# Newton steps and q/k scaling of a layer moved from VectorE to GpSimd

## The chip, the cores and the metric

The kernel runs on one core of a Trainium2 chip. The metric is the device time of one execution in microseconds (us). The core's engines work side by side, each through its own queue in order: TensorE (PE in the profile, its weight loads PEld), VectorE (DVE), ScalarE (ACT), GpSimd (POOL) and SyncE (SP, which only issues transfers). They are tied together by semaphores. GpSimd also issues transfers of its own.

## The reference, cut to what matters

Two pre-norm transformer layers over 512 tokens of width 1024, everything in fp32: layer 0 with stick-breaking attention, layer 1 with differential attention, each followed by a SwiGLU feed-forward of width 2816. The change lies in layer 1, in its two inner RMS norms.

```python
q = rms_norm(q.reshape(b, s, 8, 2, 64), q_g)     # 8 heads, two halves of 64 each
k = rms_norm(k.reshape(b, s, 8, 2, 64), k_g)
q1, q2, k1, k2 = ...                             # the halves, first 16 of 64 rotated by position
a = softmax(q1 k1 / 8) - lam * softmax(q2 k2 / 8)  # block-causal in chunks of 64
o = a @ v                                        # 128 wide per head
o = rms_norm(o, sub_g) * (1 - lam_init)
x = x + o @ w_out
```

## The kernel before

Every matrix product is done in three passes on a high and a low part of each operand (`mm3`), so that fp32 accuracy is kept. Activations lie transposed (features on partitions) between the layers; weights come in tiles of 128x1024.

Layer 1 (`diff_layer`) works in four chunks of two heads. For each chunk `qk_steps` multiplies out q and k with the tokens on partitions (`ps_nat`, four token tiles of 512 columns), ScalarE copies each into `qk_nat` (128x2048 in all) and squares it, and VectorE sums the squares of each group of 64 into `qk_ss` (128x32). Then, once for each chunk, the inverse roots of these 32 sums are found by `rsqrt`: a first guess from the bit pattern and three Newton steps of three VectorE instructions each, and the whole 128x2048 is multiplied by them (L773). GpSimd rotates the first 16 of each 64 (`rope`, L790 to L793). `v_steps` makes v for the same two heads. `head_stacks` transposes q and k of one head on TensorE (L802), splits them into high and low parts, and has GpSimd copy the k parts to the other partitions by a transfer (L334).

A head (`head`, `attend`, `weights`) does its scores in four query tiles: scores on TensorE, maximum on VectorE (L815), exponential on ScalarE (L816), the difference of the two softmaxes on VectorE (L828, two inputs in SBUF), transposes on TensorE (L358) and a split into high and low (L361, L362), then the product with v. `head_out` norms one head's output: transposes (L860), squares and sums on ScalarE (`o_sq`, L865), on VectorE a threshold factor `fin` (L873, L874) and the inverse root of four sums per partition (`rsqrt` on 128x4), their product (L877), the scaling of the transposed output from PSUM (L878), transposes back (`tb`, L887) and the split into `ohi` and `olo` (L890, L891). It is called inside the next head, behind that head's first query tile; for the eighth head after everything.

The matrix products of chunks 1 to 3 (and in heads 6 and 7 the first half of the output projection, `out_first`) are handed out in small steps between the query tiles, so that TensorE has work while a head waits. What is written is not the final order: a planner puts the instructions of each engine in an order by a simulated time line, in which earlier written work goes first when it is ready. On the chip that order is kept on each engine, whatever comes late. `tmp`, `sm` and PSUM tiles are reused in turn.

The change touches the end of `qk_steps` (L770 to L775) and the middle of `head_out` (L873 to L877), and adds a second inverse root beside `rsqrt` (L139).

Of the kernel before, what the change touches and what calls it, by code (L numbers as in the profile page):

```python
# [12 lines left out]
F32 = mybir.dt.float32  # L13
F32R = mybir.dt.float32r
BF16 = mybir.dt.bfloat16
I32 = mybir.dt.int32
AF = mybir.ActivationFunctionType
ALU = mybir.AluOpType
# [3 lines left out]
P = 128  # L22
# [4 lines left out]
TT = S // P  # L27
# [5 lines left out]
RSQRT_MAGIC = float(0x5F3759DF)  # L33
# [10 lines left out]
def trunk(  # L44
# [27 lines left out]
    V, A, G, T = nc.vector, nc.scalar, nc.gpsimd, nc.tensor  # L72

    const = ctx.enter_context(tc.tile_pool(name="const", bufs=1))
# [4 lines left out]
    sm = ctx.enter_context(tc.tile_pool(name="sm", bufs=4))  # L79
# [53 lines left out]
    def wload_kept(key):  # L133
        hi, lo = pair()
        nc.sync.dma_start(out=hi.bitcast(F32), in_=kept[key][0])
        nc.sync.dma_start(out=lo.bitcast(F32), in_=kept[key][1])
        return hi, lo

    def rsqrt(v, n):  # L139
        u = sm.tile([P, 32], F32, tag="rs_u", name="rs_u")[:, :n]  # L140
        t = sm.tile([P, 32], F32, tag="rs_t", name="rs_t")[:, :n]
        V.tensor_scalar(
            u.bitcast(I32), v.bitcast(I32), -0.5, RSQRT_MAGIC, op0=ALU.mult, op1=ALU.add
        )
        for _ in range(3):
            V.scalar_tensor_tensor(t, u, -0.5, u, op0=ALU.mult, op1=ALU.mult)
            V.tensor_tensor(t, t, v, op=ALU.mult)
            V.scalar_tensor_tensor(u, t, 1.5, u, op0=ALU.add, op1=ALU.mult)
        return u

    class Norm:
# [97 lines left out]
    def nat_steps(ws, h, evac, cols, n):  # L249
        per = 1024 // cols  # L250
        for t in range(TT):
            ts_ = slice(t * P, (t + 1) * P)
            ps = mm.tile([P, S], F32, tag="mm", name="ps_nat")[:, :cols]
            for k in range(KT):
                w = ws[k // per]
                c = slice((k % per) * cols, (k % per + 1) * cols)
                mm3(
                    ps,
                    (h[k][0][:, ts_], h[k][1][:, ts_]),
                    (w[0][:, c], w[1][:, c]),  # L260
                    k == 0,
                    k == KT - 1,
                )
                if (k + 1) % (KT // n) == 0 and k < KT - 1:
                    yield
            evac(t, ps)
            yield
# [443 lines left out]
    def diff_layer(norm, nxt):  # L711
        h = norm.h
        with ExitStack() as st:
# [14 lines left out]
            def norm_ready():  # L728
                if not norm.done:
                    norm.finish(tnp, "tn")  # L730
                    V.tensor_scalar_mul(rsv, norm.rstd, phi)
# [22 lines left out]
            def qk_steps(c, out):  # L754
                t_ = qp.tile([P, TT, S], F32, tag="qk", name="qk_nat")
                ss = sm.tile([P, 32], F32, tag="rs_v", name="qk_ss")

                def evac(t, ps):
                    norm_ready()
                    A.activation(t_[:, t], ps, AF.Copy, scale=norm.rstd[:, t : t + 1])  # L760
                    sq = tmp.tile([P, S], F32, tag="tmp", name="qk_sq")
                    A.activation(sq, t_[:, t], AF.Square)
                    V.reduce_sum(
                        ss[:, t * 8 : (t + 1) * 8],
                        sq.rearrange("p (g d) -> p g d", d=64),
                        axis=AX.X,
                    )

                yield from nat_steps([wload_kept(("wqk", c, j)) for j in range(4)], h, evac, 512, 2)
                V.tensor_scalar(ss, ss, 1.0 / 64, EPS, op0=ALU.mult, op1=ALU.add)  # L770
                u = rsqrt(ss, 32)
                f3 = t_.rearrange("p t (g d) -> p (t g) d", d=64)
                V.tensor_tensor(  # L773
                    f3, f3, u.unsqueeze(2).to_broadcast([P, 32, 64]), op=ALU.mult
                )  # L775
                for which in range(2):
                    f4 = t_[:, :, which * 256 : which * 256 + 256].rearrange(
                        "p t (g d) -> p t g d", d=64
                    )
                    ta, tb = (  # L780
                        r.unsqueeze(2).to_broadcast([P, TT, 4, ROT]) for r in rot[which]
                    )
                    mt = tmp.tile([P, S], F32, tag="tmp", name="rope")
                    m = [
                        mt[:, i * 256 : i * 256 + 256].rearrange(
                            "p (t g d) -> p t g d", t=TT, d=ROT
                        )
                        for i in range(2)
                    ]
                    G.tensor_tensor(m[1][:, :, :, 0:8], f4[:, :, :, 8:16], tb[:, :, :, 0:8], op=ALU.mult)  # L790
                    G.tensor_tensor(m[1][:, :, :, 8:16], f4[:, :, :, 0:8], tb[:, :, :, 8:16], op=ALU.mult)
                    G.tensor_tensor(m[0], f4[:, :, :, 0:ROT], ta, op=ALU.mult)
                    G.tensor_tensor(f4[:, :, :, 0:ROT], m[0], m[1], op=ALU.add)  # L793
                out.append(t_)
# [53 lines left out]
                    )  # L848
                return av, ss

            def head_out(av, ss):
                ho = raw_tile()
                ot, on = ho[:, :S], ho[:, S:]
                A.activation(ot, av, AF.Copy)
                rs = sm.tile([P, TT], F32, tag="rs1", name="rs1")
                V.reciprocal(rs, ss[:, 0])
                tp = tnp.tile([P, S], F32, tag="tn", name="tn")
                for t in range(TT):
                    o = (TT - 1 - t) * P
                    T.transpose(tp[:, t * P : (t + 1) * P], ot[:, o : o + P], ident)  # L860
                v = sm.tile([P, 32], F32, tag="rs_v", name="o_ss")[:, :TT]
                sq = tmp.tile([P, S], F32, tag="tmp", name="o_sq")
                for t in range(TT):
                    c = slice(t * P, (t + 1) * P)
                    A.activation(  # L865
                        sq[:, c],
                        tp[:, c],
                        AF.Square,
                        scale=rs[:, t : t + 1],
                        accum_out=v[:, t : t + 1],  # L870
                    )
                fin = sm.tile([P, TT], F32, tag="fin", name="fin")
                V.tensor_scalar(fin, v, thr, None, op0=ALU.is_lt)  # L873
                V.tensor_tensor(fin, fin, rs, op=ALU.mult)  # L874
                V.tensor_scalar(v, v, 1.0 / P, eps_phi, op0=ALU.mult, op1=ALU.add)
                u = rsqrt(v, TT)
                V.tensor_tensor(u, u, fin, op=ALU.mult)  # L877
                V.tensor_tensor(  # L878
                    on.rearrange("p (t d) -> p t d", d=P),
                    tp.rearrange("p (t d) -> p t d", d=P),  # L880
                    u.unsqueeze(2).to_broadcast([P, TT, P]),
                    op=ALU.mult,
                )
                tb = tnp.tile([P, S], F32, tag="tn", name="tb")
                for t in range(TT):
                    c = slice(t * P, (t + 1) * P)
                    T.transpose(tb[:, c], on[:, c], ident)  # L887
                hi = hp.tile([P, S], F32R, tag="t", name="ohi")
                lo = hp.tile([P, S], F32R, tag="t", name="olo")
                A.activation(hi, tb, AF.Copy, scale=gs)  # L890
                V.scalar_tensor_tensor(  # L891
                    lo, tb, gs, hi.bitcast(F32), op0=ALU.mult, op1=ALU.subtract
                )
                og.append((hi, lo))
# [9 lines left out]
            after = nothing  # L904
# [7 lines left out]
            for hd in range(8):  # L912
                hh = hd % 2
                c = hd // 2

                def middle():
                    if hd < 7:
                        if hh == 1:
                            flush(gens["qk", c + 1])
                        stacks.append(head_stacks(qk[(hd + 1) // 2], (hd + 1) % 2))  # L920

                def before():
                    if c > 0:
                        flush(gens["v", c])
                    if hd == 6:
                        fillers.append(last)

                q2, k2 = stacks[hd]
                av, ss = head(hh, q2, k2, lambda: vs[c], after, middle, counts[hd], before)
                after = partial(head_out, av, ss)  # L930
            after()
            flush()
            banks = [(mm, "mm"), (mm, "mm"), (scp, "sc"), (scp, "sc"), (tqp, "tq"), (tpp, "tp"), (mm, "mm"), (mm, "mm")]
# [90 lines left out]
```

## Time and profile before

| | |
|---|---|
| runs | median 1266.99 us of 3 (1265.03 to 1267.15) |
| profiled execution | 1268.86 us, span 1267.0 us |
| PE busy in the span | 1225.4 us, 97% |
| DVE / ACT / POOL busy | 732.2 / 566.8 / 101.4 us |
| chain that ended last | PE 89%, DVE 3%, issue 3%, DMA 3%, ACT 1% |

The profile shows one execution. The span runs from the first to the last instruction; 1.86 us of the execution lie around it. Times of rows are us from the start of the span, durations of single instructions in us or ns as the view says. Layer 1's attention stage, with the norms that the change touches, lies between about 640 and 890 us.

### The profile page before, as it was taken

To read this page: it belongs to the slowest core of one execution; us is meant where nothing else is said; L and a number is where in the kernel's file an instruction comes from. 1 tells how busy PE (TensorE), PEld (TensorE's weight loads), DVE (VectorE), ACT (ScalarE), POOL (GpSimd) and SP (SyncE) were. 2 spreads that over 40 slices of the span, in tenths; PEclk is the share of its full clock that TensorE was granted. 3 is DMA by queue.
4 is the path that set the end of the run, shared out by engine and by line. 5 is a ranking of instruction groups with operands and counts; after the bars stand their busy time and mean duration, and the time that the engine had idled before them with its cause. 6 is when DMAs were issued, how large, how long until landed. Compare 5 with 4: busy or idle time off the path is not lost.

```text
span 1267.0 us, 16005 instructions
## 1 busy us (share of the span) xinstructions
PE 1225.4 (97%) x5974; PEld 1024.5 (81%) x5974; DVE 732.2 (58%) x1396; ACT 566.8 (45%) x962; POOL 101.4 (8%) x169
## 2 busy tenths in 40 slices
PE   7899999989999999999999999987999999999998
PEld 6788888768888888888888998775888888888886
DVE  6467777677654555455633777885754434443442
ACT  7687977555432333233423555554442222222320
POOL 2211112001111111001101201100000000000000
PEclk9899999999999999999999999999999999999999
DMA  6966848236867776767645463531333233322222
GB/s 205 218 124 152 182 102 199 67 106 222 270 227 248 242 226 234 252 236 234 241 184 184 150 212 99 179 100 34 106 111 98 87 100 100 100 89 95 96 75 79
DMA packets 60397, 198.39 MB, mean 157 GB/s; under 512 B 8288, under 2 KB 9312, under 8 KB 60320
## 3 DMA queue, kind: packets, MB, share of 16 engines
q1 hardware_dynamic: 41760, 138.90, 34.3%
q0 software_dynamic: 18416, 58.47, 17.0%
q8 instruction: 47, 0.77, 0.2%
q14 instruction: 30, 0.25, 0.1%
q10 hardware_dynamic: 144, 0.01, 0.0%
HBM read 153.31 MB, written 35.65 MB: 149 GB/s over the span
## 4 chain that ended last, share of the span: by engine, by line
PE 89%; DVE 3%; issue 3%; DMA 3%; ACT 1%; POOL 0%; SPq 0%; DVEq 0%; POOLq 0%; ACTq 0%
PE ps_d L216 6%; PE ps_d L217 6%; PE ps_d L218 6%; PE ps_u L216 6%; PE ps_g L216 6%; PE ps_u L218 6%; PE ps_g L217 6%; PE ps_u L217 6%; PE ps_g L218 6%; PE ps_nat L216 4%; PE ps_nat L217 4%; PE ps_nat L218 4%; PE ps_o L216 2%; PE ps_o L217 2%; PE ps_o L218 2%
## 5 line engine op out<-in xcount | busy, mean ns | idle before, releaser
L109 ACT ACTIVATE whi<-wraw 128x1024 fp32r<-128x1024 f32 (+1 forms) x138 | 140.6, 1034 | 344.2 <-PE ps_d L217 82.4
L110 DVE TENSOR_TENSOR wlo<-wraw,whi 128x1024 fp32r<-128x1024 f32 (+1 forms) x138 | 164.2, 1191 | 93.7 <-ACT whi L109 47.5
L216 PE MATMUL ps_u<-hhi,whi 128*128 128x512 f32 x352 | 137.9, 392 | 3.5 <-DVE k L679 3.5
L217 PE MATMUL ps_d<-alo,whi 128*128 128x512 f32 x352 | 138.9, 396 | 0.0
L218 PE MATMUL ps_d<-ahi,wlo 128*128 128x512 f32 x352 | 138.9, 396 | 0.0
L216 PE MATMUL ps_d<-ahi,whi 128*128 128x512 f32 x352 | 138.7, 396 | 0.0
L216 PE MATMUL ps_g<-hhi,whi 128*128 128x512 f32 x352 | 137.5, 392 | 0.0
L218 PE MATMUL ps_u<-hhi,wlo 128*128 128x512 f32 x352 | 137.3, 390 | 0.0
L218 PE MATMUL ps_g<-hhi,wlo 128*128 128x512 f32 x352 | 137.2, 390 | 0.0
L217 PE MATMUL ps_g<-hlo,whi 128*128 128x512 f32 x352 | 137.1, 390 | 0.0
L217 PE MATMUL ps_u<-hlo,whi 128*128 128x512 f32 x352 | 137.0, 390 | 0.0
L216 PE MATMUL ps_nat<-whi,hhi 128*128 128x256 f32 (+1 forms) x384 | 124.1, 324 | 3.6 <-DVE k L457 3.0
L218 PE MATMUL ps_nat<-whi,hlo 128*128 128x256 f32 (+1 forms) x384 | 123.5, 322 | 0.0
L217 PE MATMUL ps_nat<-wlo,hhi 128*128 128x256 f32 (+1 forms) x384 | 122.9, 321 | 0.0
L610 DVE TENSOR_TENSOR x<-x,ps_d 128x512 f32<-128x512 f32 x48 | 32.8, 686 | 100.2 <-PE ps_d L218 100.2
L216 PEld LDWEIGHTS ps_nat<-whi,hhi 128*128 128x128 f32 x384 | 72.7, 190 | 11.0 <-DVE k L457 3.5
L216 PEld LDWEIGHTS ps_u<-hhi,whi 128*128 128x128 f32 x352 | 66.4, 189 | 17.9 <-issue 4.1
L218 PEld LDWEIGHTS ps_d<-ahi,wlo 128*128 128x128 f32 x352 | 66.1, 188 | 16.0
L216 PEld LDWEIGHTS ps_d<-ahi,whi 128*128 128x128 f32 x352 | 66.1, 188 | 16.0
L217 PEld LDWEIGHTS ps_d<-alo,whi 128*128 128x128 f32 x352 | 66.1, 188 | 15.9
L216 PEld LDWEIGHTS ps_g<-hhi,whi 128*128 128x128 f32 x352 | 66.4, 189 | 14.1 <-issue 0.2
L217 PEld LDWEIGHTS ps_g<-hlo,whi 128*128 128x128 f32 x352 | 66.2, 188 | 14.0 <-issue 0.2
(207 smaller groups left out, 2335.7 us busy)
## 6 DMA issues: line engine op xcount, KB each, us to landing
wraw<-in_wgu SPq DMA_DIRECT2D x88, 512.0 KB, 3.5
wraw<-in_wd SPq DMA_DIRECT2D x32, 512.0 KB, 3.6
k<-k POOLq DMA_DIRECT2D x32, 256.0 KB, 4.4
praw<-in_wqk SPq DMA_DIRECT2D x16, 512.0 KB, 5.1
kept_wqk<-whi POOLq DMA_DIRECT2D x16, 512.0 KB, 4.4
kept_wqk<-wlo POOLq DMA_DIRECT2D x16, 512.0 KB, 6.0
whi<-kept_wqk SPq DMA_DIRECT2D x16, 512.0 KB, 6.3
wlo<-kept_wqk SPq DMA_DIRECT2D x16, 512.0 KB, 6.2
```

What stands on the lines that cost most here:

```text
L109: A.activation(hi[:, :cols], raw[:, :cols], AF.Copy)
L110: V.tensor_tensor(lo[:, :cols], raw[:, :cols], hi.bitcast(F32)[:, :cols], op=ALU.subtract)
L216: T.matmul(ps, lh[0], rh[0], start=first, stop=False)
L217: T.matmul(ps, lh[0], rh[1], start=False, stop=False)
L218: T.matmul(ps, lh[1], rh[0], start=False, stop=last)
L610: V.tensor_tensor(x[m], x[m], ps, op=ALU.add)
```

## The change

`rsqrt_pool` takes the first guess on VectorE, then multiplies the sums by -0.5 and does three Newton steps of four two-input instructions each on GpSimd: 13 there in place of 9 on VectorE. It is used for the sums of q and k in all four chunks and in `head_out` of the first seven heads; there the two products with `fin` go to GpSimd too. The scaling of q and k (128x2048) goes to GpSimd in all chunks. The eighth head's `head_out` stays on VectorE. Two constants of 128x1 are set at the start.

```diff
+    def rsqrt_pool(v, n):
+        u = sm.tile([P, 32], F32, tag="rs_u", name="rs_u")[:, :n]
+        t = sm.tile([P, 32], F32, tag="rs_t", name="rs_t")[:, :n]
+        V.tensor_scalar(
+            u.bitcast(I32), v.bitcast(I32), -0.5, RSQRT_MAGIC, op0=ALU.mult, op1=ALU.add
+        )
+        G.tensor_tensor(v, v, half.to_broadcast([P, n]), op=ALU.mult)
+        for _ in range(3):
+            G.tensor_tensor(t, u, u, op=ALU.mult)
+            G.tensor_tensor(t, t, v, op=ALU.mult)
+            G.tensor_tensor(t, t, c15.to_broadcast([P, n]), op=ALU.add)
+            G.tensor_tensor(u, t, u, op=ALU.mult)
         return u
...
-                u = rsqrt(ss, 32)
+                u = rsqrt_pool(ss, 32)
                 f3 = t_.rearrange("p t (g d) -> p (t g) d", d=64)
-                V.tensor_tensor(
+                G.tensor_tensor(
                     f3, f3, u.unsqueeze(2).to_broadcast([P, 32, 64]), op=ALU.mult
                 )
...
-            def head_out(av, ss):
+            def head_out(av, ss, final=False):
...
-                V.tensor_tensor(fin, fin, rs, op=ALU.mult)
+                E = V if final else G
+                E.tensor_tensor(fin, fin, rs, op=ALU.mult)
                 V.tensor_scalar(v, v, 1.0 / P, eps_phi, op0=ALU.mult, op1=ALU.add)
-                u = rsqrt(v, TT)
-                V.tensor_tensor(u, u, fin, op=ALU.mult)
+                u = (rsqrt if final else rsqrt_pool)(v, TT)
+                E.tensor_tensor(u, u, fin, op=ALU.mult)
...
-                after = partial(head_out, av, ss)
+                after = partial(head_out, av, ss, hd == 7)
```

## Rows read from the trace of the kernel before

**Rows 1.** Windows: window; its length, busy us (instructions) of each engine; clock, DMA, GB/s.

```profile
690.00:800.00 110.00, 109.74 (x692) 98.78 (x691) 80.54 (x245) 62.80 (x165) 15.07 (x26) 1.00 0.56 175
800.00:862.00 62.00, 54.89 (x288) 44.96 (x287) 53.67 (x180) 32.24 (x95) 6.88 (x12) 0.94 0.34 106
862.00:890.00 28.00, 20.89 (x101) 16.32 (x100) 14.12 (x54) 10.18 (x34) 0.00 (x0) 0.89 0.18 57
810.00:820.00 10.00, 7.83 (x30) 5.48 (x31) 9.87 (x23) 4.78 (x13) 4.51 (x8) 0.83 0.09 27
```

**Rows 2.** Waits of PE in 800 to 862: total us, times, longest.

```profile
PE sc L340 <- ACT e L816: 2.8, 3, 1.8
PE sc L340 <- DMA k<-k: 1.0, 1, 1.0
...
PE tp L358 <- DVE e L828: 0.7, 1, 0.7
```

**Rows 3.** The chain that ended last, 630 to 900: start, us on the chain.

```profile
812.78 1.28 DVE qk_nat L773
```

**Rows 4.** Instructions of single lines: count, ns min/median/max, first and last start.

```profile
L148 DVE SCALAR_TENSOR_TENSOR rs_u<-rs_t,rs_u x48: 144/161/194, 22.6 to 918.2; 128x4 f32<-128x4 f32 x36, 128x32 f32<-128x32 f32 x12
L773 DVE TENSOR_TENSOR qk_nat<-qk_nat,rs_u x4: 2279/2291/2291, 664.4 to 812.7; 128x2048 f32<-128x2048 f32 x4
L828 DVE SCALAR_TENSOR_TENSOR e<-e,c,e x32: 343/540/1342, 696.0 to 869.1; 128x512 f32<-128x512 f32 x8, 128x384 f32<-128x384 f32 x8, 128x256 f32<-128x256 f32 x8, 128x128 f32<-128x128 f32 x8
```

**Rows 5.** Groups on POOL by shape: busy us, mean ns; idle before.

```profile
L334 POOL DMA_DIRECT2D k<-k x32 | 19.4, 606 | 162.0 <-DVE k L312 100.8 <-DVE c L824 19.6 <-DVE sc L814 14.5
...
L792 POOL TENSOR_TENSOR rope<-qk_nat,rot 128x256 f32<-128x256 f32 x8 | 5.8, 729 | 0.0
...
L790 POOL TENSOR_TENSOR rope<-qk_nat,rot 128x128 f32<-128x128 f32 x8 | 3.6, 452 | 80.6 <-DVE qk_nat L773 80.6
...
L1007 POOL MEMSET const-float32-1.0<- 128x1 f32 x1 | 0.1, 99 | 0.0
```

**Rows 6.** Timeline of DVE, chunk 0's norm: start, us, line, operation.

```profile
661.39 0.18 DVE L142 TENSOR_SCALAR rs_u<-qk_ss 128x32 int32<-128x32 int32 x1
...
664.42 2.29 DVE L773 TENSOR_TENSOR qk_nat<-qk_nat,rs_u 128x2048 f32<-128x2048 f32 x1
```

**Rows 7.** Timeline of POOL and of PE behind chunk 0's scaling.

```profile
666.86 0.46 POOL L790 TENSOR_TENSOR rope<-qk_nat,rot 128x128 f32<-128x128 f32 x1 [43.88 <-DVE qk_nat L773]
...
674.49 0.60 PE L802 MATMUL tqk<-ident,qk_nat 128*128 128x128 f32 x4
```

**Rows 8.** Timeline of DVE, the norms of chunks 1 and 3.

```profile
698.09 0.17 DVE L142 TENSOR_SCALAR rs_u<-qk_ss 128x32 int32<-128x32 int32 x1
...
703.31 2.29 DVE L773 TENSOR_TENSOR qk_nat<-qk_nat,rs_u 128x2048 f32<-128x2048 f32 x1
...
806.47 0.17 DVE L142 TENSOR_SCALAR rs_u<-qk_ss 128x32 int32<-128x32 int32 x1
...
812.70 2.28 DVE L773 TENSOR_TENSOR qk_nat<-qk_nat,rs_u 128x2048 f32<-128x2048 f32 x1
```

**Rows 9.** Timeline of DVE, the softmax difference beside POOL and alone; POOL's own row.

```profile
818.85 1.34 DVE L828 SCALAR_TENSOR_TENSOR e<-e,c,e 128x512 f32<-128x512 f32 x1
...
844.46 0.75 DVE L828 SCALAR_TENSOR_TENSOR e<-e,c,e 128x512 f32<-128x512 f32 x1
...
818.19 1.44 POOL L793 TENSOR_TENSOR qk_nat<-rope 128x256 f32<-128x256 f32 x2
```

**Rows 10.** Timeline of DVE, `head_out` of the sixth and of the eighth head.

```profile
849.85 0.26 DVE L873 TENSOR_SCALAR fin<-o_ss,thr 128x4 f32<-128x4 f32 x1
...
855.60 0.68 DVE L878 TENSOR_TENSOR wraw<-tn,rs_u 128x512 f32<-128x512 f32 x1
...
881.41 0.23 DVE L873 TENSOR_SCALAR fin<-o_ss,thr 128x4 f32<-128x4 f32 x1 [0.17 <-ACT o_sq L865]
...
884.18 0.69 DVE L878 TENSOR_TENSOR wraw<-tn,rs_u 128x512 f32<-128x512 f32 x1
```

More of the change, by code (lines that the diff above doesn't have):

```diff
@@ L148, in rsqrt @@
             V.scalar_tensor_tensor(u, t, 1.5, u, op0=ALU.add, op1=ALU.mult)
+        return u
+    c15 = const.tile([P, 1], F32, name="c15")
+    V.memset(c15, 1.5)
+    half = const.tile([P, 1], F32, name="half")
+    V.memset(half, -0.5)
+    def rsqrt_pool(v, n):
[10 more added lines that the diff above has]
+            G.tensor_tensor(u, t, u, op=ALU.mult)
         return u
```

## The prediction

> **What bounds the kernel now.** I read the page's engine line first: TensorE is busy 97% of the span, so an edit on VectorE can only pay where TensorE waits. The windows come next, to find where that is. From 690 to 800 TensorE is busy for 109.74 of 110.00 us while VectorE works 80.54 us [rows 1]: the products of the later chunks fill every wait of a head, and nothing taken from VectorE there shortens that stretch by itself. From 800 on, when those products run out, it is different: in 800 to 862 TensorE works 54.89 of 62.00 us and VectorE 53.67, in 810 to 820 VectorE 9.87 of 10.00 and TensorE 7.83 at a granted clock of 0.83 [rows 1]. That is the stretch in which VectorE is the fuller engine. Third, TensorE's waits in it: six rows with 6.9 us in all, the longest for the exponential, whose input is VectorE's maximum, the last for VectorE's softmax difference; only 1.0 us is a transfer [rows 2]. Fourth, the chain of waits: at 812.78 it runs 1.28 us through the scaling of q and k on VectorE, behind which a head's split waited [rows 3]. In 862 to 890 TensorE is idle 7.1 us more [rows 1], mostly in the eighth head's own output norm, which the change leaves as it is.
>
> **What the change removes from VectorE.** In each of four chunks nine Newton instructions on 128x32 at up to 0.19 us (the maximum of the line) and the scaling at 2.29 us [rows 4]: 1.7 + 2.3 = 4.0 us, 16.0 us in all. In each of seven heads nine Newton instructions and two products of the same shape at 0.16 us (the median) [rows 4], 1.8 us, 12.3 us in all. Of this, chunk 3 and the norms of heads 3 to 5 (three of them, counted from 0) lie in 800 to 862: 4.0 + 3 x 1.8 = 9.3 us of VectorE's 53.67.
>
> **What it adds to GpSimd.** The trace shows two-input operations on GpSimd of 128x128 at 0.45 us and 128x256 at 0.73 us [rows 5]. A line through both has 2.2 ns per column and 0.17 us fixed. So 128x2048 is 4.65 us, 128x32 is 0.24 us, 128x4 is 0.18 us (estimates). Bounds: for the scaling, VectorE's 2.29 us [rows 4] below and sixteen 128x128 rows, 7.2 us, above; for the small ones, the 0.10 us of a 128x1 memset and the 0.45 us of the 128x128 row [rows 5]. I take the line, since both its rows are the same operation. Per chunk that is 13 x 0.24 + 4.65 = 7.8 us, per head 15 x 0.18 = 2.7 us; in all 4 x 7.8 + 7 x 2.7 = 50 us on an engine that is busy 6.9 of 62 us in the tight stretch [rows 1]. GpSimd has room. The two constants cost nothing: two memsets of 128x1 at the start, while VectorE waits for its first data; without that cover they are 0.2 us.
>
> **The chain of q and k gets longer.** Chunk 0: the first guess ends at 661.57, the scaling on VectorE at 666.71 [rows 6]; GpSimd began the rotation 0.15 us later [rows 7], which I take as the hop between engines. New: 661.57 + 0.15 + 3.1 + 4.65 = 669.5, 2.8 us later (with the bounds, 661.57 + 0.15 + 1.3 + 2.29 = 665.3, 1.4 us earlier, to 661.57 + 0.15 + 5.85 + 7.2 = 674.8, 8.1 us later). Chunk 1: first guess until 698.26, scaling until 705.60 [rows 8], since VectorE had other work between; new 698.26 + 7.9 = 706.2, and two k transfers of 0.6 us each [rows 5] that GpSimd issues in between make it 707.4, 1.8 us later. Chunk 2 I take as chunk 1, 1.8 us. Chunk 3: 806.64 + 7.9 = 814.5 against 814.98 [rows 8], 0.4 us earlier. What this costs: chunk 0's norm starts everything in the attention, but the transposes of its q ran only at 674.49 [rows 7], some 3 us after the rotation ended (666.86 + 4 x 0.45 + 4 x 0.73 = 671.6 by rows 5), TensorE being full of v and of the next chunk meanwhile, and it stays full until 800 [rows 1]. A head that starts later uses up the filling products earlier and leaves its delay to the tail. Between none and all 2.8 us I take a quarter, 0.7 us, the same cover being there; chunks 1 and 2 start from products done early, and I take nothing. Without that cover it is 2.8 + 2 x 1.8 = 6.4 us.
>
> **The heads' norms.** On VectorE alone, the way from the threshold to the scaling takes 2.8 us (881.41 to 884.18), in the crowded stretch 5.75 us (849.85 to 855.60) [rows 10]. On GpSimd: three VectorE instructions of 0.2 us, a hop, 14 x 0.18 us, a hop, 3.4 us (bounds 2.3 and 7.2 us). So it is 0.7 us longer than VectorE undisturbed and 2.3 us shorter than in the crowd. Behind the waiting L878 on VectorE stand the next head's maxima and splits; if GpSimd comes late, they wait. Before GpSimd's norm can stand a k transfer that waits for L312.
>
> **A block between the two engines.** The softmax difference on 128x512 took 0.75 us alone, and 1.34 us when it began beside GpSimd's 1.44 us of rotation [rows 9]: it lost 0.6 us, about until GpSimd's instruction ended. The scaling on GpSimd is one instruction of 4.65 us. There are 32 such differences between 696 and 870 [rows 4], one in 5.4 us, so 0.86 of one meets each scaling, for half its length: 2.0 us of VectorE standing still, against the 2.3 us that the scaling took there. So the scaling relieves VectorE by about 0.3 us for chunk 3, and the relief in 800 to 862 shrinks from 9.3 to 7.3 us.
>
> The Trainium skill, SBUF — State Buffer, section "Who interferes with whom", states it as a rule: a VectorE instruction with two SBUF inputs and a GpSimd instruction that reads SBUF exclude each other, and the later one waits for the whole of the other. The two L828 rows agree. By that rule the worst meeting costs the whole scaling, which is the rival "block" below.
>
> **The sum.** Relief of 7.3 us on the fuller engine of 800 to 862, where TensorE's waits are 6.9 us. Half of it should reach TensorE, because the exponentials, the k transfer and the planned order keep the rest: -3.7 us. Chunk 0's later start: +0.7 us. Sum -3.0 us. The profiled execution of 1268.86 us would become 1265.9; it lies 1.9 us above the median of 1266.99, so the median becomes 1264.0 us.
>
> **Rivals.** *Block*: each of chunks 1 to 3 has one softmax difference caught for all 4.65 us, 2.4 us more than the 2.3 us taken off. In 690 to 800 the fill hides it; in chunk 3 it shows and takes 2.4 of the 3.0 us: 1266.4 us. For it: VectorE is full around 812. Against: differences are short of one per scaling. *Longer chain*: from the point at which GpSimd's small instructions take over 0.24 us, or the planner puts the transposes of a chunk later than needed, the delays of chunks 0 to 2 (6.4 us) add up head by head, and at 800 less attention is done when the fill runs out. With a relief of 3.7 us still paid that is +2.7 us, without it +6.4 us; I price it between, 1266.99 + 4.5 = 1271.5 us, slower than before. For it: heads follow one another, and each chunk's first head waits for its k. Against: TensorE idles for only 0.26 us between 690 and 800 [rows 1], and chunk 3's chain gets no longer. *Whole relief*: every VectorE-made wait of 800 to 862 goes (6.9 less the transfer's 1.0) and the clock stays up, where 0.06 of 62 us is 3.7 us: 1266.99 - 9.6 = 1257.4 us. Against: GpSimd's own answers come in only after 3.4 us.
>
> **How the numbers follow.** Forecast 0.46, with its own range 1260 to 1266; block 0.18; longer chain 0.26; whole relief 0.10. A measurement of this kernel can tell 0.2%, 2.5 us, from no change. Of the forecast 0.32 gain more than that, since less than half the relief is as likely as more, and what is left of the clock comes on top; with the whole relief faster is 0.42. Same is the block's 0.18 and the other 0.14 of the forecast, 0.32; slower 0.26. The range for 8 in 10 reaches from the whole relief to just above the longer chain, 1257 to 1273 us, and leaves out the longer chain at its dearest small instructions.
>
> **What would show it.** Right: L828 rows of 2 to 5 us beside a GpSimd scaling of about 4.65 us, small GpSimd instructions of 0.18 to 0.24 us, VectorE some 28 us less busy, TensorE idle about 3 to 4 us less between the end of the fill and the eighth head. Wrong: small GpSimd instructions at 0.4 us or more, a wait of TensorE for transposes of `qk_nat` or `wraw` between 650 and 800, or a first head starting more than 4 us later with the feed-forward shifted by as much.

## The result and the profile after

The changed kernel takes 1274.86 us (median of 8 runs, 1270.22 to 1279.76), the kernel before 1265.7 us (8 runs beside them, 1264.55 to 1268.53): a ratio of 1.0075 [1.0055, 1.0094], by which it is 9.5 us slower (9.2 by the two medians). The profiled execution took 1273.14 us, with a span of 1271.3 us.

The profiled pair shows only 4.3 us of this: the profiled run of before was 3.2 us over its median, that of after 1.7 us under. The changed kernel's runs also spread more, and longer runs tend to show a lower mean granted clock: 1270.22 us at 0.992, 1279.76 us at 0.986.

The engine line of the page after, and the shares of the chain that ended last:

```profile
PE 1229.3 (97%) x5974; PEld 1026.0 (81%) x5974; DVE 714.4 (56%) x1281; ACT 565.2 (44%) x962; POOL 152.1 (12%) x330
...
PE 88%; issue 3%; DMA 3%; DVE 3%; ACT 3%; POOL 0%; SPq 0%; DVEq 0%; POOLq 0%; ACTq 0%
```

GpSimd has 50.7 us more, as forecast (50), but by luck: the four scalings took 14.5 us where 18.6 were forecast, the small 128x4 instructions of the heads 22.2 where 18.9 were. VectorE has 17.8 us less and TensorE is at 97% as before: a lighter VectorE is plainly not a shorter kernel.

The windows of after, in the same stretches as [rows 1] (length, busy us and instructions of PE, PEld, DVE, ACT, POOL; clock, DMA, GB/s):

```profile
690.00:800.00 110.00, 106.66 (x656) 94.22 (x655) 68.55 (x181) 56.82 (x148) 38.15 (x99) 1.00 0.57 177
800.00:862.00 62.00, 57.70 (x318) 47.76 (x317) 51.86 (x145) 36.90 (x109) 25.45 (x73) 0.97 0.36 111
862.00:890.00 28.00, 19.37 (x100) 15.40 (x99) 14.37 (x48) 10.15 (x35) 3.10 (x15) 0.97 0.12 38
810.00:820.00 10.00, 9.59 (x48) 7.38 (x49) 9.41 (x31) 5.02 (x16) 7.38 (x25) 1.00 0.54 192
```

Against [rows 1], TensorE idles 3.34 instead of 0.26 us between 690 and 800, where nothing was expected to show, and less between 800 and 862. But fixed windows mislead here, because the work has moved: the same instant now shows earlier work. So take stages that are bounded by events: from the first matmul of the layer's norm (`ps_ss`) to the first score, from there to the last product of chunks 1 to 3 (the fill), from there to the last score, and on to the next norm. First before:

```profile
643.68:690.40 46.72, 46.61 (x260) 40.34 (x259) 15.84 (x40) 13.25 (x23) 5.73 (x10) 1.00 0.44 148
690.40:804.00 113.60, 113.34 (x722) 102.39 (x721) 84.44 (x259) 66.50 (x175) 15.07 (x26) 1.00 0.55 172
804.00:866.10 62.10, 54.48 (x279) 44.09 (x278) 52.59 (x177) 31.41 (x94) 6.88 (x12) 0.95 0.31 100
866.10:915.20 49.10, 42.50 (x186) 33.95 (x185) 31.92 (x72) 22.75 (x47) 0.00 (x0) 0.93 0.24 76
```

The same four stages after:

```profile
644.08:697.50 53.42, 52.78 (x297) 45.80 (x296) 13.88 (x34) 15.93 (x26) 12.76 (x26) 1.00 0.47 160
697.50:809.40 111.90, 108.89 (x685) 96.92 (x684) 73.31 (x196) 61.48 (x167) 38.64 (x101) 1.00 0.52 159
809.40:867.80 58.40, 53.93 (x279) 43.44 (x278) 48.83 (x140) 32.16 (x98) 23.83 (x69) 0.97 0.34 108
867.80:919.50 51.70, 42.67 (x186) 34.19 (x186) 30.97 (x62) 23.15 (x48) 3.10 (x15) 0.93 0.22 72
```

The first score comes 6.7 us later (53.42 against 46.72). TensorE isn't idle meanwhile: it does 52.78 us of work there, with products of the next chunks. It has that much less to fill with afterwards, and idles 3.0 us in the fill (before 0.3). The two later stages together are 1.1 us shorter (110.1 against 111.2) and the four together 3.9 us longer.

TensorE's waits in the fill, after (total us, times, longest); before there is a single wait of 0.3 us, for a weight:

```profile
PE sc L359 <- DMA k<-k: 1.4, 1, 1.4
PE tn L879 <- ACT wraw L873: 0.7, 1, 0.7
PE tb L907 <- DVE wraw L898: 0.6, 1, 0.6
PE sc L359 <- ACT e L835: 0.2, 1, 0.2
```

The longest is chunk 2's first head waiting for its k at 798.70, with the weights' transfers of the output projection on the queues: k was issued at 790.25 and 791.25 and took 8.4 us to land (before, the first of the same two took 7.4 us and no score waited).

GpSimd in chunk 0 after; it answers to [rows 6, 7]:

```profile
662.04 0.24 POOL L162 TENSOR_TENSOR qk_ss<-qk_ss,half 128x32 f32<-128x32 f32 x1 [38.62 <-DVE rs_u L159]
662.25 0.23 POOL L164 TENSOR_TENSOR rs_t<-rs_u 128x32 f32<-128x32 f32 x1
662.56 0.25 POOL L165 TENSOR_TENSOR rs_t<-rs_t,qk_ss 128x32 f32<-128x32 f32 x1
...
666.12 3.63 POOL L792 TENSOR_TENSOR qk_nat<-qk_nat,rs_u 128x2048 f32<-128x2048 f32 x1
669.83 0.46 POOL L809 TENSOR_TENSOR rope<-qk_nat,rot 128x128 f32<-128x128 f32 x1
```

The 13 small instructions take 4.08 us (662.04 to 666.12) where 3.1 were forecast, and the scaling 3.63 where 4.65 were. The errors cancel: the rotation begins 2.97 us later than in [rows 7], forecast 2.8. So the chain was right up to here. TensorE's first transposes of q in chunk 0, 674.49 in [rows 7], now:

```profile
678.95 0.60 PE L821 MATMUL tqk<-ident,qk_nat 128*128 128x128 f32 x4
```

That is 4.5 us later, and the first score 7.1 us later on the span's clock. TensorE did not wait for q: the planned order puts more products ahead of these transposes, 193 since the start of the layer's norm where it had been 175, and 276 ahead of the first score where it had been 239.

### The profile page after: what moved, and what is told of

It is laid out like the page before. It is cut to its first block, busy times and chain, and to the rows that moved or that the text cites. A ratio compares the mean times of both kernels' runs of the same rounds, so it can differ in the third digit from the quotient of the medians.

```text
span 1271.3 us, 16047 instructions
## 1 busy us (share of the span) xinstructions
PE 1229.3 (97%) x5974; PEld 1026.0 (81%) x5974; DVE 714.4 (56%) x1281; ACT 565.2 (44%) x962; POOL 152.1 (12%) x330
## 4 chain that ended last, share of the span: by engine, by line
PE 88%; issue 3%; DMA 3%; DVE 3%; ACT 3%; POOL 0%; SPq 0%; DVEq 0%; POOLq 0%; ACTq 0%
PE ps_d L236 6%; PE ps_d L235 6%; PE ps_d L237 6%; PE ps_u L235 6%; PE ps_g L235 6%; PE ps_u L236 6%; PE ps_g L236 6%; PE ps_u L237 6%; PE ps_g L237 6%; PE ps_nat L235 4%; PE ps_nat L236 4%; PE ps_nat L237 4%; PE ps_o L235 2%; PE ps_o L236 2%; PE ps_o L237 2%
## 5 line engine op out<-in xcount | busy, mean ns | idle before, releaser
L236 PEld LDWEIGHTS ps_u<-hlo,whi 128*128 128x128 f32 x352 | 66.4, 189 | 14.0 <-issue 0.2
```

The lines of the kernel that those rows point to most:

```text
L236: T.matmul(ps, lh[0], rh[1], start=False, stop=False)
```

## The experiments

Ratios are to the kernel before, run beside each on the same chip. Where a diff is against the changed kernel it says "after". **Late** is how much later the first score comes after the start of the layer's norm than before (46.7 us), **last chunk** the same for the first transposes of chunk 3 (177.5 us before), **fill idle** TensorE's idle time from the first score to the last product of chunks 1 to 3; all from each one's profile, to about 0.1 us. The rows without "before" are versions of the changed kernel.

| kernel | ratio [95%] | late | last chunk | fill idle |
|---|---|---|---|---|
| before | 1 | 0 | 0 | 0.3 |
| after, again | 1.0078 [1.0061, 1.0094] | 7.0 | 7.2 | 2.8 |
| chunk 0 on VectorE | 0.9991 [0.9981, 1.0001] | 0.1 | 0.8 | 0.4 |
| and all scalings there | 1.0004 [0.9993, 1.0016] | 0.0 | 2.0 | 0.4 |
| before, c0 rotation of q on VectorE | 1.0005 [0.9994, 1.0016] | -1.5 | -0.2 | 0.2 |
| chunk 0 and its q rotation on VectorE | 1.0013 [1.0001, 1.0026] | -1.5 | 1.1 | 0.2 |
| heads only | 1.0030 [1.0018, 1.0043] | 0.0 | 5.4 | 2.4 |
| before, half delay in chunk 0 | 1.0035 [1.0021, 1.0049] | 3.5 | 2.6 | 1.5 |
| before, delay in chunk 2 | 1.0036 [1.0022, 1.0049] | 0.0 | 5.5 | 1.3 |
| heads and chunk 3 | 1.0037 [1.0022, 1.0051] | 0.1 | 4.8 | 2.7 |
| chunks 1 to 3 only | 1.0048 [1.0033, 1.0064] | 0.1 | 1.1 | 2.2 |
| chunk 0 on VectorE, delayed | 1.0058 [1.0040, 1.0076] | 4.6 | 6.1 | 2.5 |
| before, delay in chunk 0 | 1.0064 [1.0048, 1.0080] | 4.9 | 7.8 | 4.5 |
| of chunk 0 only the Newton steps on GpSimd | 1.0070 [1.0048, 1.0092] | 3.6 | 2.3 | 1.5 |
| of chunk 0 only the scaling on GpSimd | 1.0073 [1.0053, 1.0093] | 3.5 | 3.6 | 2.9 |
| q and k only | 1.0081 [1.0062, 1.0101] | 7.2 | 8.6 | 2.9 |
| before, double delay in chunk 0 | 1.0101 [1.0077, 1.0124] | 11.3 | 15.8 | 6.3 |

### The changed kernel again, and one part at a time

The changed kernel without an edit, beside the next three:

> The changed kernel itself, again, as the control of the others and for a second profile of it. All theories: 1.0055 to 1.0094 of before, and a first score of the first head near 698 us (691 before). If the spread of its runs (1270 to 1280) comes from TensorE's clock, a profile with a longer time has the lower mean clock, and the difference lies behind 690 us.

1275.23 us, 1.0078: the loss repeats.

Chunk 0's norm and scaling back on VectorE (after):

```diff
-                u = rsqrt_pool(ss, 32)
+                u = (rsqrt if c == 0 else rsqrt_pool)(ss, 32)
...
-                G.tensor_tensor(
+                (V if c == 0 else G).tensor_tensor(
```

> The change, but chunk 0's inverse root and scaling stay on VectorE. Theory 'late start': the first head's first score came 7 us later (698.2 against 691.1) because chunk 0's norm is longer on GpSimd, and a head chain that starts late ends late; with chunk 0 back it starts near 691, and the time falls by 5 to 9 us, to 0.999 to 1.003 of before. Theory 'heads' norms' (the Newton steps of head_out on GpSimd answer late, TensorE waits for tb and the tail): no fall, 1.005 to 1.009. Theory 'block' (the 3.63 us scaling on GpSimd holds up VectorE's softmax differences): chunk 0 meets none of these, so 1.005 to 1.009 too.

1264.52 us, 0.9991: the whole loss is gone, 10.7 us against the changed kernel, by one chunk of four. Chunks 1 to 3 and seven heads are still on GpSimd; in this version they cost nothing and bring nothing that this can tell.

All heads' norms on VectorE, q and k as changed (after):

```diff
-                after = partial(head_out, av, ss, hd == 7)
+                after = partial(head_out, av, ss, True)
```

> Only q and k's part of the change: inverse root and scaling of all four chunks on GpSimd, all eight heads' norms on VectorE. 'Late start': the loss stays, 1.005 to 1.010. 'Heads' norms': the loss goes, 0.998 to 1.002. 'Block': the loss stays.

1276.27 us, 1.0081: the part on q and k alone brings the whole loss.

The norms of q and k on VectorE, the heads as changed (after):

```diff
-                u = rsqrt_pool(ss, 32)
+                u = rsqrt(ss, 32)
...
-                G.tensor_tensor(
+                V.tensor_tensor(
```

> Only the heads' part: Newton steps and the two products of heads 0 to 6 on GpSimd, q and k's norm on VectorE as before. 'Late start': no loss, or a gain from the 12 us taken from VectorE, 0.997 to 1.001, first score near 691. 'Heads' norms': the loss stays, 1.005 to 1.009. 'Block': no loss.

1269.95 us, 1.0030, outside the ranges of all three theories: the heads alone cost too, although the parts don't add up (the version with chunk 0 undone has all these heads on GpSimd and loses nothing). What is late here is chunk 2's first head, which waits 1.69 us for its k at 790.32. GpSimd's timeline just before, and VectorE's split of that k:

```profile
779.95 0.20 POOL L167 TENSOR_TENSOR rs_u<-rs_t,rs_u 128x4 f32<-128x4 f32 x1
780.23 0.20 POOL L897 TENSOR_TENSOR rs_u<-rs_u,fin 128x4 f32<-128x4 f32 x1
780.74 0.62 POOL L353 DMA_DIRECT2D k<-k  x1 [0.31 <-issue]
```

```profile
779.20 0.68 DVE L331 TENSOR_TENSOR k<-tqk,k 64x512 fp32r<-64x512 f32 x1
```

k was split at 779.88; its transfer, on GpSimd's queue, went out at 780.74 behind the last of the 15 instructions of the head's norm, 0.86 us after the split where it had been 0.30 before. That is the smaller part of the wait: the transfer also took 9.5 us to land, where it had taken 7.4. Two of the output projection's weight transfers had gone out ahead of it; before, none had. The transfers of k with their weights, before and here (median of two):

```profile
k<-k POOLq DMA_DIRECT2D x2, 256.0 KB, 8.1
```

```profile
k<-k POOLq DMA_DIRECT2D x2, 256.0 KB, 10.3
```

### Is it GpSimd, or only that chunk 0 is late?

The kernel before, with a multiplication by ones on VectorE that does nothing but delay chunk 0 by its length (2.28 us):

```diff
+                if c == 0:
+                    V.tensor_tensor(
+                        f3, f3, ones[:, :64].unsqueeze(1).to_broadcast([P, 32, 64]), op=ALU.mult
+                    )
```

> The kernel before, nothing on GpSimd, with chunk 0's q and k multiplied once more by a tile of ones on VectorE (2.3 us, no change of the numbers): only chunk 0's norm is later. 'Late start': a first score some 2.3 us later or more, and the time 2 to 6 us up, 1.002 to 1.005, without any GpSimd work. 'GpSimd itself' (its instructions hold up VectorE or its queue): no loss, 0.998 to 1.002.

1273.3 us, 1.0064 (8.1 us) with nothing of the change in it, more than 'late start' expected (1.002 to 1.005). The delay explains the sign, its length not yet the size.

The two halves of chunk 0's norm, each back on VectorE alone (after):

```diff
-                u = rsqrt_pool(ss, 32)
+                u = (rsqrt if c == 0 else rsqrt_pool)(ss, 32)
```

> The change, with chunk 0's inverse root back on VectorE and its scaling still on GpSimd. The 13 dependent GpSimd instructions took 4.08 us (662.04 to 666.12) against 2.8 us from the first guess to the scaling before, the scaling 3.63 against 2.29. 'Late start': the chip's own chain is 1.7 us later than before instead of 3.0, so some 55% of the loss stays if the planner's order follows the chain: 1.001 to 1.005. If the planner is what delays the head and holds GpSimd's small instructions for far dearer than they are, nearly all goes: 0.998 to 1.001.

```diff
-                G.tensor_tensor(
+                (V if c == 0 else G).tensor_tensor(
```

> The counterpart: chunk 0's inverse root on GpSimd, its scaling back on VectorE. By the chip's chain about 1.5 us later than before: 1.001 to 1.005. If the planner holds the 128x2048 scaling on GpSimd for far dearer than its 3.63 us, nearly all the loss goes: 0.998 to 1.001. The first score's time tells: 691 before, 698 to 700 in the change.

1275.39 us, 1.0073 with the Newton steps of chunk 0 back on VectorE and 1272.87 us, 1.0070 with its scaling back; both ranges (up to 1.005) were missed. Undoing half the delay gives back next to nothing, which speaks against a price in strict proportion.

Chunk 0 and all heads on VectorE, chunks 1 to 3 as changed (the two edits of the second version, and all heads as in the third):

> Chunks 1 to 3 on GpSimd, chunk 0 and all heads' norms on VectorE. The run with the heads' part alone was 0.30% slower, the one with both parts but without chunk 0 0.09% faster. If the parts add, this is the good part alone: 0.995 to 0.998. If a plan's luck in the tail decides (the tail from the last score to the last output transposes was 18 to 22 us in the runs so far, without a pattern by part), 0.998 to 1.004.

1271.23 us, 1.0048, above both ranges, though the first score is in its old place. The same delay as above in chunk 2 (before, with `if c == 2`):

> The kernel before with the same 2.3 us multiplication by ones that cost 0.64% in chunk 0, now in chunk 2. 'Late start': the first score stays 47.4 us behind the layer's norm sums, the time within 0.998 to 1.003. 'Any other plan is worse' (the kernel before has a lucky order, and every edit of this region loses some 0.6%): 1.004 to 1.008.

1269.46 us, 1.0036 (4.6 us), twice the delay's length and between the two ranges: a later chunk's delay is paid as well, about half as dearly.

An earlier start, by q's rotation of chunk 0 on VectorE beside k's on GpSimd, in the kernel before:

```diff
+                    R = V if c == 0 and which == 0 else G
-                    G.tensor_tensor(m[1][:, :, :, 0:8], f4[:, :, :, 8:16], tb[:, :, :, 0:8], op=ALU.mult)
+                    R.tensor_tensor(m[1][:, :, :, 0:8], f4[:, :, :, 8:16], tb[:, :, :, 0:8], op=ALU.mult)
...
```

> The kernel before with chunk 0's rotation of q (four instructions) on VectorE, so that it runs beside GpSimd's rotation of k: chunk 0's chain gets some 1 to 3 us shorter. 'Late start' with the sign turned: first score before 46 us behind the norm sums and 1 to 4 us faster, 0.997 to 0.999. 'Any other plan is worse': 1.003 to 1.008.

and the same in the version with chunk 0 undone:

> The best so far (the change with chunk 0's norm on VectorE, 0.9991) and chunk 0's rotation of q on VectorE as well. 'Late start': faster than both kernels, 0.995 to 0.998. 'Any other plan is worse': 1.000 to 1.006.

1265.98 us, 1.0005, and 1267.51 us, 1.0013. The first score comes 1.5 us earlier and nothing is gained, against what 'late start' expected: chunk 3's transposes stay where they were (-0.2 and 1.1 us). So in these runs the start binds when it is late, and not when it is early.

The version with chunk 0 undone, and the scaling of the other chunks on VectorE too (after):

```diff
-                u = rsqrt_pool(ss, 32)
+                u = (rsqrt if c == 0 else rsqrt_pool)(ss, 32)
...
-                G.tensor_tensor(
+                V.tensor_tensor(
```

> The 0.9991 kernel with the scaling of chunks 1 to 3 back on VectorE too; their inverse roots stay on GpSimd. 'Block': softmax differences of up to 3.3 us go (none over 1.4 us), and the time falls by 1 to 3 us, 0.996 to 0.999. If the relief of VectorE by 2.3 us per chunk was worth more than the block costs, it rises: 1.000 to 1.003.

1266.05 us, 1.0004: taking the long GpSimd instruction away brings nothing, so the block between the two engines costs nothing that shows here.

### Does the price grow with the delay?

At this point the price of chunk 0's delay, 8 us for 2.3, could be the delay carried from head to head, or the price of another planned order. Half, and twice the delay, in the kernel before:

```diff
+                if c == 0:
+                    V.tensor_tensor(
+                        f3[:, :16], f3[:, :16], ones[:, :64].unsqueeze(1).to_broadcast([P, 16, 64]), op=ALU.mult
+                    )
```

> The kernel before, with an added multiplication by ones of half of q and k of chunk 0 on VectorE (about 1.15 us). Theory (the delay of chunk 0 is carried from head to head to the end of the attention): half of the loss of the full multiplication, about +4 us, ratio 1.003, first score some 2 us later after the norm. Rival (any change of the first head's place makes the planner lay out another order, and its price does not depend on the size): either no loss (1.000) or the full one (1.006).

```diff
+                for _ in range(2 if c == 0 else 0):
+                    V.tensor_tensor(
+                        f3, f3, ones[:, :64].unsqueeze(1).to_broadcast([P, 32, 64]), op=ALU.mult
+                    )
```

> The kernel before, with two multiplications by ones of all of q and k of chunk 0 on VectorE (about 4.6 us). Theory (carried delay): twice the loss of one, +13 to +17 us, ratio 1.010 to 1.013, first score 7 to 10 us later. Rival (the price of another order): about the loss of one, 1.006 to 1.008.

1270.17 us, 1.0035 (4.4 us) and 1278.93 us, 1.0101 (12.8 us). With the single delay's 8.1 us the price grows with the dose: neither none nor the same. The rival of a price that doesn't depend on the size falls. The first two stages of these kernels, half, single and double:

```profile
640.60:690.80 50.20, 50.10 (x277) 43.22 (x277) 17.02 (x41) 13.96 (x23) 5.73 (x10) 1.00 0.46 152
690.80:802.10 111.30, 109.82 (x700) 98.65 (x699) 79.90 (x248) 63.46 (x167) 15.15 (x25) 1.00 0.50 164
```

```profile
640.10:691.70 51.60, 51.42 (x287) 44.40 (x286) 18.54 (x42) 15.29 (x25) 5.72 (x10) 1.00 0.45 150
691.70:807.50 115.80, 111.35 (x691) 99.45 (x692) 81.86 (x254) 63.24 (x169) 15.55 (x26) 0.99 0.53 162
```

```profile
638.90:696.90 58.00, 57.06 (x333) 50.04 (x332) 26.34 (x59) 17.01 (x28) 5.74 (x10) 1.00 0.52 174
696.90:812.20 115.30, 108.97 (x643) 96.03 (x644) 74.93 (x239) 60.71 (x163) 14.73 (x25) 0.96 0.46 137
```

Read the first column of each pair, then PE. The first score is 3.5, 4.9 and 11.3 us late, TensorE fills nearly all of that, and then idles 1.5, 4.5 and 6.3 us in the fill, where before it idled 0.3. With the double delay the granted clock of the fill is 0.96, against 1.00 without delay. The cost is 1.1 to 1.7 times what the first score is late; the changed kernel's 9.5 us for 6.7 lies between, the two halves of chunk 0's norm lie outside (some 9 us for 3.5). TensorE's waits in the fill, single and double delay:

```profile
PE sc L340 <- DMA k<-k: 2.0, 1, 2.0
PE sc L340 <- ACT e L820: 0.9, 1, 0.9
PE ps_nat L216 <- DVE v1l L740: 0.7, 1, 0.7
```

```profile
PE sc L340 <- DMA k<-k: 3.6, 3, 2.5
PE sc L340 <- ACT e L820: 2.0, 2, 1.0
```

The changed kernel's longest wait, k of a head, is the longest here too, with no norm on GpSimd.

The version with chunk 0 undone, with the delay put into it (the multiplication of the single delay, added to that version's chunk 0):

> The kernel after with chunk 0's norm on VectorE, but with a multiplication by ones of all of q and k of chunk 0 there (about 2.3 us), so that GpSimd has none of chunk 0's norm and chunk 0 is as late as in the slower kernels. Theory (carried delay): the loss comes back, +0.6 to +0.8%, ratio 1.005 to 1.008. Rival (the loss came from GpSimd's own work in chunk 0): stays near 0.9991, at most 1.002.

1272.93 us, 1.0058: the delay alone brings most of the loss back into the changed kernel, with chunk 0's norm on VectorE.

The norms of chunks 0 to 2 on VectorE; chunk 3 and seven heads as changed (after):

```diff
-                u = rsqrt_pool(ss, 32)
+                u = (rsqrt_pool if c == 3 else rsqrt)(ss, 32)
...
-                G.tensor_tensor(
+                (G if c == 3 else V).tensor_tensor(
```

> The kernel after, with the norms of chunks 0 to 2 back on VectorE; on GpSimd stay chunk 3's norm and scaling and the first seven heads' norms. Theory (carried delay): no chunk before the last starts later, so nothing is carried and the relief of VectorE between 800 and 862 us shows: -3 to 0 us, ratio 0.998 to 1.000, like the version with only chunk 0 undone. Rival (heads on GpSimd cost by themselves, as the heads alone did): +3 to +4 us, 1.0025 to 1.003.

1269.8 us, 1.0037: here the theory missed and the rival was nearer. No chunk before the last has a longer chain, and yet the relief doesn't show; as with the heads alone, TensorE waits 2.0 us for a k in the fill and the last chunk is 4.8 us late. The relief that the prediction reckoned with isn't there even where nothing early is delayed on purpose.

No version beat the kernel before by more than its measurement can tell.

## Why the prediction was wrong

**The failed step is the price of chunk 0's later start.** "Between none and all 2.8 us I take a quarter, 0.7 us, the same cover being there", says the prediction. The cover was read from TensorE being full until 800 [rows 1]. It is full: but the fill is a fixed stock, and a head that starts later doesn't find it again. The prediction said so itself ("uses up the filling products earlier and leaves its delay to the tail") and then priced it at a quarter. Measured: the 2.97 us at the rotation become 6.7 us at the first score, since the order of TensorE is laid out around the later chain, 7.2 us at the last chunk's transposes, and about 9.5 us in the time. The term is not 0.7 but of the size of the whole loss, which undoing chunk 0 takes away (0.9991, 10.7 us less than the changed kernel), a delay without any GpSimd brings (1.0064) and brings back (1.0058), and half and double doses scale (1.0035, 1.0101).

**The relief of VectorE was not worth 3.7 us.** The instructions went as forecast and GpSimd had the room, though VectorE's busy time fell by 17.8 us and not by 28. The durations of what was taken away do add up to 28.0 us, and those of all VectorE instructions fell by 25.3 (788.7 to 763.4); in the traces these instructions overlap (788.7 us of durations in 732.2 us of busy time), so that taking one out frees less than its duration. The version that keeps all of the relief from chunks 1 to 3 and the heads and has the old start is 1.1 us faster, its interval reaching from 2.4 us faster to no change, and the one with chunk 3 and the heads is 4.7 us slower. "Half of it should reach TensorE" rested on TensorE's waits of 6.9 us [rows 2]; removing VectorE's work in that stretch doesn't shorten them by half, and the products that the later start moves away from it also change what is left there. The version with the old start shows it without that, in its stage from the last product of chunks 1 to 3 to the last score:

```profile
802.60:863.00 60.40, 52.88 (x283) 42.20 (x282) 50.08 (x144) 34.45 (x107) 21.50 (x60) 1.00 0.38 111
```

VectorE works 2.5 us less there than before (50.08 against 52.59), and TensorE idles 7.5 us as it did (7.6): next to nothing of the relief reached its waits. The stage is 1.7 us shorter at a granted clock of 1.00 against 0.95, nearly all of it in TensorE's own work. In the changed kernel's profile the two later stages are 1.1 us shorter in all, and that is no measure of relief, since the start moved work ahead of them.

**The rival "longer chain"** named the mechanism, delays that add up head by head until the fill runs out, at +4.5 us; the measured loss is about twice that. Its two conditions divide: the small instructions did exceed its 0.24 us, not in length but from start to start (0.32 us); and the planner did put chunk 0's transposes later than the chain needs, 4.6 us behind the rotation's end (674.32 to 678.95) where it had been 3.1. One sign that the prediction gave for being wrong came true in its first half: the first head starts over 4 us later (7.1 us), the next norm, of the feed-forward, 4.3 us (919.5 against 915.2). Another, a wait of TensorE for `qk_nat` or `wraw`, came as 0.6 and 0.7 us for `wraw`.

**The costs on GpSimd.** The two groups after that answer to the estimates (busy us, mean ns; idle before):

```profile
L792 POOL TENSOR_TENSOR qk_nat<-qk_nat,rs_u 128x2048 f32<-128x2048 f32 x4 | 14.5, 3626 | 0.3
...
L167 POOL TENSOR_TENSOR rs_u<-rs_t,rs_u 128x32 f32<-128x32 f32 x12 | 3.0, 252 | 0.9
```

The line through 128x128 and 128x256 [rows 5] was 28% too dear for 128x2048. For 128x32 it was nearly right (0.24 forecast, 0.24 to 0.27 measured), but a dependent instruction starts only 0.32 us after the one ahead, so thirteen take 4.1 and not 3.1 us.

**The heads' norms** were to take 3.4 us from the threshold to the scaling. VectorE after, a head on GpSimd and the eighth, on VectorE:

```profile
787.84 0.23 DVE L892 TENSOR_SCALAR fin<-o_ss,thr 128x4 f32<-128x4 f32 x1 [0.16 <-ACT o_sq L884]
...
795.62 0.69 DVE L898 TENSOR_TENSOR wraw<-tn,rs_u 128x512 f32<-128x512 f32 x1
...
885.73 0.23 DVE L892 TENSOR_SCALAR fin<-o_ss,thr 128x4 f32<-128x4 f32 x1 [3.49 <-ACT o_sq L884]
888.50 0.69 DVE L898 TENSOR_TENSOR wraw<-tn,rs_u 128x512 f32<-128x512 f32 x1
```

7.8 us here, 4.8 to 6.2 us in the other six, 5.8 us on average. On VectorE the same seven took 4.3 to 9.5 us, 6.2 us on average; the 5.75 us of [rows 10] is one of them. So the gain in the crowd is 0.4 us a head where 2.3 were forecast. The k transfers on the same queue are part of it, as the prediction feared, and lose by it: in this head's norm stand two of 0.62 us, and the first went out 0.65 us after its split, where it had been 0.30.

**The block** was there and was small. The softmax difference in all, after, against 18.2 us before (569 ns on average):

```profile
L847 DVE SCALAR_TENSOR_TENSOR e<-e,c,e 128x512 f32<-128x512 f32 (+3 forms) x32 | 19.7, 615 | 0.6
```

1.5 us more over the whole kernel, where 2.0 us for each scaling were forecast: the planned order seldom puts the two side by side. Where it does, as in the version with chunk 0 undone, the difference waits until GpSimd is done:

```profile
703.65 3.29 DVE L847 SCALAR_TENSOR_TENSOR e<-e,c,e 128x256 f32<-128x256 f32 x1
```

```profile
703.04 3.62 POOL L792 TENSOR_TENSOR qk_nat<-qk_nat,rs_u 128x2048 f32<-128x2048 f32 x1
```

Both end within 0.3 us of each other (706.94 and 706.66). And that version has the lowest median of all.

**What stays open.** The five kernels that lose at most 0.13% (0.9991 to 1.0013, the one before among them) idle 0.2 to 0.4 us in the fill; all others idle 1.3 us or more. That holds as well for the four whose first score is not late (1.0030 to 1.0048). There the traces say where the wait is: chunk 2's first head waits 1.3 to 2.0 us for its k. This transfer was issued while four or five weight transfers were under way, the output projection's among them, and took 9.1 to 9.8 us, against 7.4 us before, with one of v's under way. But in the version with chunk 0 undone it took 9.2 us too, and there TensorE waited only 0.3 us. No run moved these transfers, so that they cost the time (3.8 to 6.1 us) is not shown. The price isn't strictly in proportion: half of chunk 0's norm on GpSimd costs as much as all of it. What the planned order adds by itself, some 0.3 to 0.5%, wasn't separated from the delays, since every edit makes another order. And the profiles don't hold the whole loss: from the layer's norm to the next norm the changed kernel's two profiles are 3.9 and 4.8 us longer than the one of before, where the ratios give 9.5 and 9.9. Up to the layer's norm TensorE does the same 3015 instructions in the same order in all the kernels, and took between 638.5 and 645.5 us over the 18 profiles; with one or two profiles of a kernel the other half of the loss can't be placed.

## What to carry to other kernels

An engine that is full with filler is not cover for a late start: the filler is a fixed stock, and what is used ahead of the first consumer is missing behind it. Price a delay of the first link of a chain of stages at no less than its whole length; in this kernel it cost about three to four times that (8.1 us for 2.28 added, 9.5 for 2.97), and an earlier start brought nothing. Before moving work to an idle engine, ask which of its instances stand at the head of the chain, and leave those where they are. Moving the others brought no gain here either that the measurement can tell: time taken from a busy engine counts only where another engine's wait ends on it.

## What the runs showed of the hardware

- One 128x2048 product with a broadcast operand took 3.63 us on GpSimd and 2.29 us on VectorE [rows 4].
- Small dependent instructions on GpSimd, some 0.20 us long on 128x4 and 0.25 us on 128x32, follow each other at 0.28 and 0.32 us.
- A softmax difference on VectorE took up to 4.12 us, in the version with only q and k on GpSimd, against 0.75 us alone [rows 9]. The Trainium skill, SBUF — State Buffer, section "Who interferes with whom", has the later of two such instructions wait for the whole of the other; the pair at 703 us agrees, with 3.29 us.
